# Making the weight sums of a seven-product FFN on the vector engine instead of by accumulating transfers

## The chip, the cores and the metric

The kernel runs on one core of a Trainium2 chip. That core has a matrix engine (PE, which also loads its own weights, shown as PEld), a vector engine (DVE), an activation engine (ACT), a general engine (POOL), a sequencer that mainly starts transfers (SP), and 16 DMA engines that move data between HBM and the on-chip memory. The metric is the device time of one execution in microseconds.

## The reference

Two residual layers over a sequence of 512 tokens with 1024 channels, each followed by a dense SwiGLU FFN. The FFN is the part that matters here:

```
def swiglu_layer(x, norm_g, w_gate_up, w_down):
    h = rmsnorm(x, norm_g)
    g, u = jnp.split(h @ w_gate_up, 2, axis=-1)     # 1024 -> 2 x 2816
    return x + (jax.nn.silu(g) * u) @ w_down        # 2816 -> 1024
```

All in float32. The first layer mixes by a recurrence and a state-space model, the second by attention; the change touches neither.

## The kernel before, in words

Channels lie on the 128 partitions and tokens along the free axis, so that an activation tile is 128x512. To reach float32 accuracy each operand is split into a high part (a cast on ACT, line 93) and a low part (a subtraction on DVE, line 94), and each product is three matmuls: low by high, high by low, high by high (lines 163 to 165). Both parts are tiles of up to 128x1024.

The FFN has 22 hidden tiles. They are worked off in three parts, of 8, 7 and 7 tiles (`HID`); after each part comes its down-projection of eight output tiles (lines 838 to 842). The first five hidden tiles of a layer are made by ordinary products. Tiles 5 to 21, in this text *pairs* (a gate tile and an up tile), are made by `seven`: the pair of weight tiles and the activations are seen as 2x2 blocks, and seven block products replace eight. So each layer has a stretch of 3 pairs and two stretches of 7 pairs, and there are 34 pairs in all. A block product is 4 x 3 = 12 matmuls of 256 columns, so a pair is 84 matmuls.

The weight side of the seven products needs, beside the gate tile itself (`a1`) and the right half of the up tile (`a22`), four sums: `s13` is a tile with two sums, and `s24` is made from `s13` and the gate tile by two additions (lines 143 and 144). In the kernel before, the two sums of `s13` are made on the way in: the left half of the up tile is loaded twice, into both halves of the tile (line 132), and then two transfers started by POOL add another block on top (lines 135 and 136). The gate tile comes by line 133 and `a22` by line 134. Each of the four weight tiles is then split into high and low by ACT and DVE.

`weight` makes the tiles ahead of their use: for pairs, four tiles ahead, which is one pair. Where the tiles lie is set by two rings (`ring`): four buffers for raw tiles inside an FFN (a pair takes two of them: the gate tile and `s13`), five for split tiles. `s24` has a single buffer, `a22` has two.

In `seven` the order of the products on PE is: B11 with `a1`; then the sixth product of the pair before (`end1`); T2 with `s24`; the seventh of the pair before (`end2`); T1 and T3 with `s13`; B21 with `a1`. Results are taken out of the accumulators by ACT and DVE between them: `s` and `m5` by ACT, `u2`, `u3`, `tg`, `tu` by DVE (lines 787 to 813). T3 is accumulated onto T2, so PE may start T3 only when `u2` (line 792) has read T2; in the same way the seventh product waits for `u3` (line 799).

Each engine works through its own queue strictly in order. The order inside a queue is not that of the source but is chosen by a list scheduler when the program is built, which also puts transfers where it expects their buffers to be free. An instruction of a queue that has to wait holds up everything behind it.

Of the kernel before, what the change touches and what calls it, by code (L numbers as in the profile page):

```python
# [10 lines left out]
F32 = mybir.dt.float32  # L11
# [3 lines left out]
ALU = mybir.AluOpType  # L15
AX = mybir.AxisListType

P = 128
# [7 lines left out]
KF = FF // P  # L26
# [3 lines left out]
NSTD = 5  # L30
# [31 lines left out]
def trunk(ctx: ExitStack, tc: tile.TileContext, a):  # L62
    nc = tc.nc
    mm = nc.tensor.matmul
    V, S, G = nc.vector, nc.scalar, nc.gpsimd
# [18 lines left out]
    WMAX = D  # L84
# [7 lines left out]
    def split(src, hi, lo, eng=V):  # L92
        S.copy(hi, src)  # L93
        eng.tensor_tensor(out=lo, in0=src, in1=hi.bitcast(F32), op=ALU.subtract)  # L94
# [4 lines left out]
    lent = {"stage": None, "pool": None, "raw": 0, "split": 0}  # L99

    def ring(what, stage):

        own, more = (NRAW, 1) if what == "raw" else (NSPL, 2)
        names = (("raw", F32),) if what == "raw" else (("whi", F32R), ("wlo", F32R))
        pool, bufs = wp, own
        if stage is not None and stage == lent["stage"]:
            lent[what] += 1
            if lent[what] % (own + more) >= own:
                pool, bufs = lent["pool"], more
        return [pool.tile([P, WMAX], dt, tag=n, bufs=bufs, name=n) for n, dt in names]  # L110

    parts = {}

    def emit(j):
        src, n, kind, stage = specs[j]
        HW = WMAX // 2
        if kind == "plain":
            raw, = ring("raw", stage)
            hi, lo = ring("split", stage)
            step = n if j else n // 4  # L120
            for c in range(0, n, step):
                nc.sync.dma_start(out=raw[:, c:c + step], in_=src[:, c:c + step])
                split(raw[:, c:c + step], hi[:, c:c + step], lo[:, c:c + step], G if src.tensor.name in on_pool else V)
        elif kind == "a1":

            g, u = src
            fp = lent["pool"]
            raw, = ring("raw", stage)
            s13, = ring("raw", stage)
            a22 = fp.tile([P, HW], F32, tag="a22", name="a22", bufs=2)  # L130
            for z in range(2):
                nc.sync.dma_start(out=s13[:, z * HW:(z + 1) * HW], in_=u[:, :HW])
            nc.sync.dma_start(out=raw, in_=g)
            nc.sync.dma_start(out=a22, in_=u[:, HW:])
            nc.gpsimd.dma_start(out=s13[:, :HW], in_=u[:, HW:], accum_op=ALU.add)  # L135
            nc.gpsimd.dma_start(out=s13[:, HW:], in_=g[:, :HW], accum_op=ALU.add)
            parts.update(raw=raw, s13=s13, a22=a22)
            hi, lo = ring("split", stage)
            split(raw, hi, lo)
        elif kind == "s24":  # L140
            raw, s13 = parts["raw"], parts["s13"]
            t = lent["pool"].tile([P, WMAX], F32, tag="s24", name="s24", bufs=1)
            V.tensor_tensor(out=t[:, :HW], in0=s13[:, :HW], in1=raw[:, :HW], op=ALU.add)  # L143
            V.tensor_tensor(out=t[:, HW:], in0=t[:, :HW], in1=raw[:, HW:], op=ALU.add)
            hi, lo = ring("split", stage)
            split(t, hi, lo)
        elif kind == "s13":
            hi, lo = ring("split", stage)
            split(parts["s13"], hi, lo)
        else:  # L150
            hi, lo = (lent["pool"].tile([P, HW], F32R, tag=f"a22{z}", name=f"a22{z}", bufs=1) for z in "hl")
            split(parts["a22"], hi, lo)
        w_of[j] = (hi, lo)

    def weight(i):
        while emitted[0] < len(specs) and emitted[0] <= i + (AHEAD if specs[emitted[0]][2] == "plain" else 4):
            emitted[0] += 1
            emit(emitted[0] - 1)
        return w_of.pop(i, None)
# [69 lines left out]
    def slot(i, dtype):  # L229
        return [xp.tile([P, T], dtype, tag=f"x{z}{i}", name=f"x{z}{i}") for z in "hl"]  # L230
# [79 lines left out]
    with ExitStack() as rctx:  # L310
# [63 lines left out]
        for c in range(NT):  # L374
# [33 lines left out]
            out=adt.rearrange("p (c h) -> p c h", c=NT),  # L408
            in0=dt.rearrange("p (c h) -> p c h", c=NT),
            scalar=-1.0,  # L410
            in1=ea.rearrange("p (o h) -> p o h", o=1).to_broadcast([P, NT, H]),
# [24 lines left out]
        for g in range(2):  # L436
# [7 lines left out]
            for c in range(NT):  # L444
                s = slice(c * P, (c + 1) * P)
# [3 lines left out]
                out=t.rearrange("p (c l) -> p c l", c=NT), in0=ps.rearrange("p (c l) -> p c l", c=NT),  # L449
                in1=tri.rearrange("p (o l) -> p o l", o=1).to_broadcast([P, NT, P]), op=ALU.mult,  # L450
# [245 lines left out]
        op = rctx.enter_context(tc.tile_pool(name="op", bufs=1))  # L696
# [9 lines left out]

    HOMES = [("F", i) for i in range(5)] + [("S", i) for i in (8, 9, 10, 11, 4, 5, 6, 7)] + [("F", i) for i in range(5)] + [("S", i) for i in (8, 9, 10, 11)]

# [4 lines left out]
    def ffn(norm, idx, after):  # L717
        l, gu, dn = idx
        HT = T // 2
        with ExitStack() as fctx:  # L720
            fp = fctx.enter_context(tc.tile_pool(name="fp", bufs=1))
# [47 lines left out]
            def finish(m, tu):  # L769
                z, i = HOMES[m]  # L770
                hi, lo = slot(i, F32R) if z == "S" else [fp.tile([P, T], F32R, tag=f"a{y}{i}", name=f"a{y}") for y in "hl"]
                split(tu, hi, lo)
                act[m] = (hi, lo)

            def small(tag):
                return fp.tile([P, HT], F32, tag=tag, name=tag, bufs=2)

            def seven(m, last):

# [2 lines left out]
                r1, r2 = (pa.tile([P, T], F32, tag="pa", name="ps_r")[:, :HT] for _ in range(2))  # L782
                r3 = pm.tile([P, T], F32, tag="pm", name="ps_r3")[:, :HT]
                s, u2, u3, m5 = small("s"), small("u2"), small("u3"), small("m5")
                a1 = weight(gu[m]["a1"])
                product(r1, a1, 0, "B11", True)
# [64 lines left out]
    with ExitStack() as actx:  # L851
# [11 lines left out]
        for w, (gn, rn, scale) in enumerate((("q_gain", "q_rope", 0.125), ("k_gain", "k_rope", 1.0))):  # L863
            g = am.tile([P, 1], F32, name=f"gain{w}", bufs=1)
# [301 lines left out]
```

## Time and profile before

| | |
|---|---|
| median of 3 runs | 1334.52 us (1334.01 to 1335.09) |
| the profiled execution | 1333.48 us, of which the span from first to last instruction is 1331.6 us |
| PE busy | 1296.0 us, 97% of the span |
| DVE busy | 928.1 us, 70% |
| ACT busy | 645.6 us, 48% |
| POOL busy | 180.0 us, 14% |
| moved by DMA | 153.46 MB, mean 115 GB/s |

Busy shares are averages over stages with different limits. A busy PE only says that matmuls were in flight; whether it lost time is seen by comparing a stretch's length with that of the same work where nothing was waited for. In the rows below, `raw`, `s`, `u` and `a` are tile names without their numbers: `raw` is any tile of the raw ring (the gate tile and `s13`), `s<-raw` on line 143 is the first addition for `s24`, `wlo` is the low part of a weight tile, and `a` stands for `a22`.

### The profile page before, as it was taken

The numbers are of one execution on the slowest core, as the hardware profiler recorded it, in microseconds if no ns is written. First come the engines' busy times: TensorE is split into PE (matmuls) and PEld (weight loads), VectorE is DVE, ScalarE is ACT, GpSimd is POOL, SyncE is SP. The second block draws the span as 40 slices with busy tenths as digits, with TensorE's granted clock in tenths as the row PEclk, the third lists the DMA queues.
The fourth block names the chain that finished last, engine by engine and source line by source line (L and its number), as shares of the span: only waits on it lengthen the run. The fifth ranks groups of instructions, "written<-read, shape, count | busy, mean of one in ns | idle before, by whom it ended". The sixth has DMA issues, their size and how long they took to land.

```text
span 1331.6 us, 18948 instructions
## 1 busy us (share of the span) xinstructions
PE 1296.0 (97%) x7346; PEld 1113.9 (84%) x7346; DVE 928.1 (70%) x1550; ACT 645.6 (48%) x1012; POOL 180.0 (14%) x178
## 2 busy tenths in 40 slices
PE   7999989999999999999999999999999999999998
PEld 6877767788889889889888877877878989889997
DVE  6886789975688558747764666777789746765772
ACT  6743858443455325424443467546654514433540
POOL 0000000000010111011104453354201011111100
PEclk9999989999999999999999999999999999999999
DMA  7323322532454646564632321221245554565541
GB/s 242 112 80 94 96 74 70 163 111 91 143 131 109 173 109 164 162 143 111 158 96 80 95 79 33 64 79 49 66 132 120 158 127 127 144 162 131 148 128 56
DMA packets 58154, 153.46 MB, mean 115 GB/s; under 512 B 6464, under 2 KB 7232, under 8 KB 57936
## 3 DMA queue, kind: packets, MB, share of 16 engines
q1 hardware_dynamic: 48272, 134.43, 32.7%
q0 software_dynamic: 9792, 17.83, 8.6%
q8 instruction: 57, 0.93, 0.3%
q14 instruction: 33, 0.27, 0.1%
HBM read 150.10 MB, written 2.13 MB: 114 GB/s over the span
## 4 chain that ended last, share of the span: by engine, by line
PE 81%; DVE 8%; ACT 4%; DMA 4%; issue 2%; SPq 0%; POOL 0%; DVEq 0%; ACTq 0%; POOLq 0%
PE ps_pr L163 15%; PE ps_pr L164 15%; PE ps_pr L165 15%; PE ps_r L765 6%; PE ps_r L767 6%; PE ps_r L766 6%; DMA raw<-in_w_gu 4%; PE ps_qkv L905 3%; PE ps_qkv L906 3%; PE ps_qkv L907 3%; DVE wlo L94 3%; PE ps_pT L1017 1%; ACT s L996 1%; PE ps_s L988 1%; PE ps_o L1025 1%
## 5 line engine op out<-in xcount | busy, mean ns | idle before, releaser
L93 ACT CAST whi<-raw 128x1024 fp32r<-128x1024 f32 (+2 forms) x223 | 227.4, 1022 | 327.1 <-PE ps_pr L165 208.8
L163 PE MATMUL ps_pr<-xh,wlo 128*128 128x512 f32 x704 | 279.7, 397 | 13.0 <-DVE wlo L94 12.3
L164 PE MATMUL ps_pr<-xl,whi 128*128 128x512 f32 x704 | 277.7, 394 | 0.6 <-DVE xl L245 0.6
L165 PE MATMUL ps_pr<-xh,whi 128*128 128x512 f32 x704 | 276.6, 393 | 0.0
L94 DVE TENSOR_TENSOR wlo<-raw,whi 128x1024 fp32r<-128x1024 f32 (+2 forms) x191 | 224.4, 1181 | 42.1 <-ACT whi L93 41.2
L163 PEld LDWEIGHTS ps_pr<-xh,wlo 128*128 128x128 f32 x704 | 133.5, 190 | 42.4 <-DVE wlo L94 13.1
L164 PEld LDWEIGHTS ps_pr<-xl,whi 128*128 128x128 f32 x704 | 133.4, 189 | 29.7 <-DVE xl L245 1.8
L165 PEld LDWEIGHTS ps_pr<-xh,whi 128*128 128x128 f32 x704 | 133.3, 189 | 28.6 <-issue 0.6
L840 DVE TENSOR_TENSOR x<-ps_pr,x 128x512 f32<-128x512 f32 x48 | 33.2, 691 | 96.8 <-PE ps_pr L165 96.6
L94 POOL TENSOR_TENSOR wlo<-raw,whi 128x1024 fp32r<-128x1024 f32 x32 | 78.0, 2438 | 167.1 <-ACT whi L93 167.1
L135 POOL DMA_DIRECT2D raw<-in_w_gu x34 | 30.4, 893 | 482.8 <-DMA raw<-in_w_gu 191.8
L765 PE MATMUL ps_r<-xh,wlo 128*128 128x256 f32 x272 | 77.1, 283 | 0.0
L767 PE MATMUL ps_r<-xh,whi 128*128 128x256 f32 x272 | 77.0, 283 | 0.0
L766 PE MATMUL ps_r<-xl,whi 128*128 128x256 f32 x272 | 77.0, 283 | 0.0
L907 PE MATMUL ps_qkv<-whi,xh 128*128 128x512 f32 x192 | 75.5, 393 | 0.0
L905 PE MATMUL ps_qkv<-whi,xl 128*128 128x512 f32 x192 | 75.4, 392 | 0.0
L906 PE MATMUL ps_qkv<-wlo,xh 128*128 128x512 f32 x192 | 75.3, 392 | 0.0
L93 ACT CAST whi<-s 128x1024 fp32r<-128x1024 f32 x34 | 35.8, 1052 | 71.2 <-PE ps_pr L165 37.4
L143 DVE TENSOR_TENSOR s<-raw 128x512 f32<-128x512 f32 x34 | 23.5, 691 | 56.3 <-DMA raw<-in_w_gu 54.5
L163 PE MATMUL ps_pr<-ah,wlo 128*128 128x512 f32 x160 | 62.3, 389 | 0.0
L164 PE MATMUL ps_pr<-al,whi 128*128 128x512 f32 x160 | 62.3, 389 | 0.0
L165 PE MATMUL ps_pr<-ah,whi 128*128 128x512 f32 x160 | 62.2, 389 | 0.0
(372 smaller groups left out, 3074.7 us busy)
## 6 DMA issues: line engine op xcount, KB each, us to landing
raw<-in_w_gu SPq DMA_DIRECT2D x54, 512.0 KB, 3.6
raw<-in_w_in SPq DMA_DIRECT2D x35, 512.0 KB, 3.6
raw<-in_w_gu SPq DMA_DIRECT2D x68, 256.0 KB, 3.4
raw<-in_w_gu POOLq DMA_DIRECT2D x68, 256.0 KB, 5.5
raw<-in_w_dn SPq DMA_DIRECT2D x32, 448.0 KB, 3.9
raw<-in_w_qkv SPq DMA_DIRECT2D x24, 512.0 KB, 3.5
a<-in_w_gu SPq DMA_DIRECT2D x34, 256.0 KB, 3.9
raw<-in_w_out SPq DMA_DIRECT2D x16, 512.0 KB, 3.6
```

The source lines that it names most:

```text
L93: S.copy(hi, src)
L94: eng.tensor_tensor(out=lo, in0=src, in1=hi.bitcast(F32), op=ALU.subtract)
L163: mm(ps, lhsT=wl[ws], rhs=xh[xs], start=start, stop=False)
L164: mm(ps, lhsT=wh[ws], rhs=xl[xs], start=False, stop=False)
L165: mm(ps, lhsT=wh[ws], rhs=xh[xs], start=False, stop=stop)
L765: mm(ps, lhsT=wl[:, c:c + P], rhs=fh, start=first and k == 0, stop=False, skip_group_check=not first)
L766: mm(ps, lhsT=wh[:, c:c + P], rhs=fl, start=False, stop=False, skip_group_check=not first)
L767: mm(ps, lhsT=wh[:, c:c + P], rhs=fh, start=False, stop=k == 3, skip_group_check=not first)
L840: V.tensor_tensor(out=x[m], in0=ps, in1=x[m], op=ALU.add)
L905: mm(pss[t], lhsT=xl[:, ts_], rhs=wh[:, cols], start=(k == 0), stop=False)
L906: mm(pss[t], lhsT=xh[:, ts_], rhs=wl[:, cols], start=False, stop=False)
L907: mm(pss[t], lhsT=xh[:, ts_], rhs=wh[:, cols], start=False, stop=(k == KD - 1))
```

## The change

The two accumulating transfers per pair go, and so do the two loads of the up tile's left half and the separate load of its right half. Instead the up tile is loaded whole by one transfer, into the ring place that `s13` had. `s13` becomes a tile of its own with a single buffer, and DVE makes its two sums by two more additions of 128x512 in front of the two that make `s24`. The five `F` homes of activation tiles become four, and `u2`, `u3` and `m5` have one buffer each instead of two.

```diff
@@ emit, kind "a1" @@
             raw, = ring("raw", stage)
-            s13, = ring("raw", stage)
-            a22 = fp.tile([P, HW], F32, tag="a22", name="a22", bufs=2)
-            for z in range(2):
-                nc.sync.dma_start(out=s13[:, z * HW:(z + 1) * HW], in_=u[:, :HW])
+            up, = ring("raw", stage)
             nc.sync.dma_start(out=raw, in_=g)
-            nc.sync.dma_start(out=a22, in_=u[:, HW:])
-            nc.gpsimd.dma_start(out=s13[:, :HW], in_=u[:, HW:], accum_op=ALU.add)
-            nc.gpsimd.dma_start(out=s13[:, HW:], in_=g[:, :HW], accum_op=ALU.add)
-            parts.update(raw=raw, s13=s13, a22=a22)
+            nc.sync.dma_start(out=up, in_=u)
+            a22 = up[:, HW:]
+            s13 = lent["pool"].tile([P, WMAX], F32, tag="s13", name="s13", bufs=1)
+            parts.update(raw=raw, s13=s13, a21=up[:, :HW], a22=a22)
@@ emit, kind "s24" @@
+            V.tensor_tensor(out=s13[:, :HW], in0=a21, in1=a22, op=ALU.add)
+            V.tensor_tensor(out=s13[:, HW:], in0=a21, in1=raw[:, :HW], op=ALU.add)
             t = lent["pool"].tile([P, WMAX], F32, tag="s24", name="s24", bufs=1)
             V.tensor_tensor(out=t[:, :HW], in0=s13[:, :HW], in1=raw[:, :HW], op=ALU.add)
             V.tensor_tensor(out=t[:, HW:], in0=t[:, :HW], in1=raw[:, HW:], op=ALU.add)
@@ homes and small results @@
-    HOMES = [("F", i) for i in range(5)] + ... + [("F", i) for i in range(5)] + ...
+    HOMES = [("F", i) for i in range(4)] + ... + [("F", i) for i in range(3)] + ... + [("F", i) for i in range(4)]
-                return fp.tile([P, HT], F32, tag=tag, name=tag, bufs=2)
+                return fp.tile([P, HT], F32, tag=tag, name=tag, bufs=2 if tag == "s" else 1)
```

In the changed kernel the gate tile is loaded by line 129, the up tile by line 130, and the four additions are lines 139, 140, 142 and 143; `u2`, `u3` and `tg` are lines 794, 801 and 809.

On DVE, the place is the first layer's first 7-pair stretch, where its fifth pair ends and its sixth begins; here the tiles of the seventh are made (`raw_4755` is its `s13`, `raw_4754` its gate tile). `a22l` is the low part of the fifth pair's `a22`, `xl6` an activation's low part, and `wlo_4698` belongs to the sixth pair's `s13`. Before:

```order
L94 TENSOR_TENSOR a22l_4594<-a22_4486,a22h_4593 128x512
L143 TENSOR_TENSOR s24_4794<-raw_4755,raw_4754 128x512
L94 TENSOR_TENSOR xl6_4694<-tu_4476,xh6_4693 128x512
L799 TENSOR_TENSOR u3_4617<-ps_r_4613,s_4615 128x256
L144 TENSOR_TENSOR s24_4794<-s24_4794,raw_4754 128x512
L800 TENSOR_TENSOR tu_4611<-m5_4618,u3_4617 128x256
L94 TENSOR_TENSOR wlo_4798<-s24_4794,whi_4797 128x1024
L94 TENSOR_TENSOR wlo_4698<-raw_4620,whi_4697 128x1024
L807 TENSOR_TENSOR tg_4610<-ps_r3_4614,u2_4616 128x256
L94 TENSOR_TENSOR wlo_4764<-raw_4754,whi_4763 128x1024
L792 TENSOR_TENSOR u2_4751<-ps_r_4748,s_4750 128x256
```

The same place on DVE after the change; `raw_4737` is the seventh pair's whole up tile, `raw_4736` its gate tile, `raw_4471` the up tile of the fifth, `s13_4607` the sums of the sixth:

```order
L94 TENSOR_TENSOR a22l_4578<-raw_4471,a22h_4577 128x512
L94 TENSOR_TENSOR xl7_4676<-tu_4462,xh7_4675 128x512
L801 TENSOR_TENSOR u3_4601<-ps_r_4597,s_4599 128x256
L802 TENSOR_TENSOR tu_4595<-m5_4602,u3_4601 128x256
L94 TENSOR_TENSOR wlo_4680<-s13_4607,whi_4679 128x1024
L139 TENSOR_TENSOR s13_4740<-raw_4737 128x512
L809 TENSOR_TENSOR tg_4594<-ps_r3_4598,u2_4600 128x256
L140 TENSOR_TENSOR s13_4740<-raw_4737,raw_4736 128x512
L142 TENSOR_TENSOR s24_4774<-s13_4740,raw_4736 128x512
L94 TENSOR_TENSOR wlo_4742<-raw_4736,whi_4741 128x1024
L143 TENSOR_TENSOR s24_4774<-s24_4774,raw_4736 128x512
L794 TENSOR_TENSOR u2_4733<-ps_r_4730,s_4732 128x256
```

The first addition that needs a transfer has moved behind `u3`, `tu` and the split of the sixth pair's `s13`, whose single buffer it writes; all four additions now stand in front of `u2`, where before the second one stood in front of `u3` already.

On SP, the transfers of the same stretch's last pairs; `L132` fills the two halves of an `s13` tile. Before:

```order
L133 DMA raw_4484<-in_w_gu 128x1024
L134 DMA a22_4351<-in_w_gu 128x512
L132 DMA raw_4485<-in_w_gu 128x512 x2
L132 DMA raw_4620<-in_w_gu 128x512 x2
L134 DMA a22_4486<-in_w_gu 128x512
L133 DMA raw_4754<-in_w_gu 128x1024
L133 DMA raw_4619<-in_w_gu 128x1024
L134 DMA a22_4621<-in_w_gu 128x512
L132 DMA raw_4755<-in_w_gu 128x512 x2
```

After, where `L129` is a gate tile and `L130` an up tile, for the last four pairs:

```order
L129 DMA raw_4337<-in_w_gu 128x1024
L129 DMA raw_4470<-in_w_gu 128x1024
L130 DMA raw_4338<-in_w_gu 128x1024
L130 DMA raw_4471<-in_w_gu 128x1024
L129 DMA raw_4603<-in_w_gu 128x1024
L129 DMA raw_4736<-in_w_gu 128x1024
L130 DMA raw_4604<-in_w_gu 128x1024
L130 DMA raw_4737<-in_w_gu 128x1024
```

Two transfers per pair stand on SP where there were four, and POOL, which had two per pair, has none in the FFN. An up tile's place in the ring becomes free only when the right half of the up tile two pairs earlier has been split (`a22l`), so its transfer starts there.

## Rows read from the trace of the kernel before

**Rows 1.** The page: busy time, share of the span and instructions.

```profile
PE 1296.0 (97%) x7346; PEld 1113.9 (84%) x7346; DVE 928.1 (70%) x1550; ACT 645.6 (48%) x1012; POOL 180.0 (14%) x178
```

**Rows 2.** Pair stretches: length; busy PE, PEld, DVE, ACT, POOL; clock, DMA share, GB/s.

```profile
413.20:443.43 30.23, 30.23 (x253) 30.23 (x252) 23.53 (x34) 17.00 (x26) 0.00 (x0) 1.00 0.43 126
486.98:560.20 73.22, 71.05 (x589) 70.64 (x588) 55.10 (x85) 37.94 (x61) 7.04 (x8) 1.00 0.58 150
598.31:673.69 75.38, 72.27 (x589) 70.97 (x588) 54.87 (x85) 37.49 (x61) 7.07 (x8) 1.00 0.51 131
1027.63:1057.87 30.24, 30.24 (x254) 30.23 (x253) 23.36 (x34) 16.98 (x26) 1.77 (x2) 1.00 0.53 143
1101.41:1177.27 75.86, 72.96 (x590) 72.14 (x589) 55.08 (x85) 37.40 (x61) 7.07 (x8) 0.98 0.54 137
1215.37:1289.69 74.32, 71.82 (x589) 70.80 (x588) 55.02 (x85) 38.02 (x61) 7.06 (x8) 1.00 0.58 144
```

**Rows 3.** Waits: who for whom, us in total, times, longest.

```profile
PE ps_r L765 <- DVE wlo L94: 7.5, 4, 2.5
PE ps_r L765 <- DVE u L799: 1.7, 2, 1.3
...
DVE s L143 <- DMA raw<-in_w_gu: 54.5, 21, 5.4
```

**Rows 4.** Timeline of DVE: start, us, instruction, idle before and releaser.

```profile
634.49 0.68 DVE L94 TENSOR_TENSOR a22l<-a,a22h 128x512 fp32r<-128x512 f32 x1
640.54 0.69 DVE L143 TENSOR_TENSOR s<-raw 128x512 f32<-128x512 f32 x1 [5.36 <-DMA raw<-in_w_gu]
...
641.75 0.42 DVE L799 TENSOR_TENSOR u<-ps_r,s 128x256 f32<-128x256 f32 x1
...
643.02 2.35 DVE L94 TENSOR_TENSOR wlo<-raw,whi 128x1024 fp32r<-128x1024 f32 x2
```

**Rows 5.** Timeline of POOL at the same place.

```profile
634.95 0.88 POOL L135 DMA_DIRECT2D raw<-in_w_gu  x1 [18.91 <-DVE tu L813]
```

**Rows 6.** Timeline of PE at the same place.

```profile
642.22 0.39 PE L765 MATMUL ps_r<-t10h,a22l 128*128 128x256 f32 x1 [1.27 <-DVE u L799]
...
645.42 0.39 PE L765 MATMUL ps_r<-t00h,wlo 128*128 128x256 f32 x1 [1.50 <-DVE wlo L94]
```

**Rows 7.** Busy time by stretch, behind the longest stop of PE.

```profile
1149.40:1152.80 3.40, 3.40 (x17) 3.19 (x17) 2.15 (x5) 0.91 (x3) 0.00 (x0) 0.51 0.76 240
```

**Rows 8.** Timeline of DVE in a pair of the first 7-pair stretch.

```profile
525.17 0.68 DVE L144 TENSOR_TENSOR s<-s,raw 128x512 f32<-128x512 f32 x1
525.77 0.41 DVE L799 TENSOR_TENSOR u<-ps_r,s 128x256 f32<-128x256 f32 x1
526.10 0.68 DVE L94 TENSOR_TENSOR xl<-tu,xh 128x512 fp32r<-128x512 f32 x1
...
527.04 2.35 DVE L94 TENSOR_TENSOR wlo<-raw,whi 128x1024 fp32r<-128x1024 f32 x2
529.31 0.41 DVE L807 TENSOR_TENSOR tg<-ps_r,u 128x256 f32<-128x256 f32 x1
```

**Rows 9.** Groups of DVE by form: count, busy us, mean ns, idle before.

```profile
L94 DVE TENSOR_TENSOR wlo<-raw,whi 128x1024 fp32r<-128x1024 f32 x155 | 188.2, 1220 | 33.9 <-ACT whi L93 33.4
...
L144 DVE TENSOR_TENSOR s<-s,raw 128x512 f32<-128x512 f32 x34 | 23.3, 685 | 0.3
```

**Rows 10.** DMA issues: queue, count, KB each, median us to landing.

```profile
raw<-in_w_gu SPq DMA_DIRECT2D x68, 256.0 KB, 3.4
raw<-in_w_gu POOLq DMA_DIRECT2D x68, 256.0 KB, 5.5
```

**Rows 11.** Line 133, the gate tiles of the pairs, 512 KB each.

```profile
DMA to landing us min/median/max: 3.4/3.9/6.6
```

**Rows 12.** Busy time by stretch: the ordinary hidden tiles of each layer.

```profile
363.00:413.20 50.20, 50.20 (x227) 41.69 (x227) 44.37 (x74) 25.35 (x37) 7.47 (x7) 1.00 0.52 133
970.00:1027.63 57.63, 56.96 (x256) 46.33 (x255) 50.55 (x82) 29.65 (x42) 5.04 (x5) 1.00 0.43 118
```

More of the change, by code (lines that the diff above doesn't have):

```diff
@@ L126, in emit @@
             g, u = src
-            fp = lent["pool"]
             raw, = ring("raw", stage)
-            s13, = ring("raw", stage)
-            a22 = fp.tile([P, HW], F32, tag="a22", name="a22", bufs=2)
-            for z in range(2):
-                nc.sync.dma_start(out=s13[:, z * HW:(z + 1) * HW], in_=u[:, :HW])
+            up, = ring("raw", stage)
             nc.sync.dma_start(out=raw, in_=g)
-            nc.sync.dma_start(out=a22, in_=u[:, HW:])
-            nc.gpsimd.dma_start(out=s13[:, :HW], in_=u[:, HW:], accum_op=ALU.add)
-            nc.gpsimd.dma_start(out=s13[:, HW:], in_=g[:, :HW], accum_op=ALU.add)
-            parts.update(raw=raw, s13=s13, a22=a22)
+            nc.sync.dma_start(out=up, in_=u)
+            a22 = up[:, HW:]
+            s13 = lent["pool"].tile([P, WMAX], F32, tag="s13", name="s13", bufs=1)
+            parts.update(raw=raw, s13=s13, a21=up[:, :HW], a22=a22)
             hi, lo = ring("split", stage)
@@ L140, in emit @@
         elif kind == "s24":
-            raw, s13 = parts["raw"], parts["s13"]
+            raw, s13, a22 = parts["raw"], parts["s13"], parts["a22"]
+            a21 = parts["a21"]
+            V.tensor_tensor(out=s13[:, :HW], in0=a21, in1=a22, op=ALU.add)
+            V.tensor_tensor(out=s13[:, HW:], in0=a21, in1=raw[:, :HW], op=ALU.add)
             t = lent["pool"].tile([P, WMAX], F32, tag="s24", name="s24", bufs=1)
@@ L705, in trunk @@
             norm.feed(m)
-    HOMES = [("F", i) for i in range(5)] + [("S", i) for i in (8, 9, 10, 11, 4, 5, 6, 7)] + [("F", i) for i in range(5)] + [("S", i) for i in (8, 9, 10, 11)]
+    NF = NSTD - 1
+    HOMES = [("F", i) for i in range(NF)] + [("S", i) for i in (8, 9, 10, 11, 4, 5, 6, 7)] + [("F", i) for i in range(3)]
+    HOMES += [("S", i) for i in (8, 9, 10, 11)] + [("F", i) for i in range(NF)]
+    assert len(HOMES) >= KF
     def ffn(norm, idx, after):
```

## The prediction, made before the changed kernel ran

> **What bounds the kernel now.** I read the busy times first. PE is busy for 97% of the span, DVE for 70%, POOL for 14% [rows 1]. The change takes no matmul away, so it can only win where PE stands still, and the busy times by stretch show where. A 3-pair stretch takes 30.23 us and its PE is never idle [rows 2], so a pair costs PE 10.08 us and seven pairs 70.56. The four 7-pair stretches take 73.22, 75.38, 75.86 and 74.32 us: they lose 2.66, 4.82, 5.30 and 3.76 us, together 16.54. The stretches of ordinary tiles ahead of them leave PE idle for 0.67 us, all of it in the second layer [rows 12]. So 16.5 us, 1.2% of the run, is what stands to be won.
>
> The waits name the cause from the other end. PE waits for `wlo` (7.5 us) and for `u3` (1.7 us), both made by DVE; DVE, before the first addition for `s24`, waits 54.5 us in 21 waits for a transfer into the raw ring [rows 3]. One place shows the chain. POOL starts an accumulating transfer at 634.95 [rows 5], as late as that because its destination had to be free and then loaded. DVE has finished `a22l` at 635.2 and stands until 640.54 behind that transfer, 5.36 us; `u3`, for which PE's result has long been ready, is queued behind the addition and comes at 641.75, and the low parts of two weight tiles at 643.02 [rows 4]. PE stops twice, until 642.22 for `u3` and until 645.42 for `wlo` [rows 6]. So PE stops not because DVE is full but because DVE's queue stands still behind a late transfer. Once the stop is long it costs twice: after the longest one, near 1149.4, the granted clock is 0.51 for 3.40 us, that is, the lower level of 1.2 GHz, and 17 matmuls run there where 28 would at 0.12 us each [rows 7]. That is 17 x 0.12 = 2.04 us of work, so 1.4 of the 5.30 us of that stretch are clock.
>
> **The change part by part.** *Transfers.* The chain for one `s13` is now a load (median 3.4 us) and then an accumulation (5.5 us) [rows 10], 8.9 us in a row after the buffer is free. It becomes one 512 KB load; the gate tiles are of that size and land in 3.9 us in the middle, 3.4 to 6.6 [rows 11]. That is 5.0 us less. But the buffer comes free later: the up tile's right half is split last of the four tiles, and the next-but-one pair's load starts only behind that `a22l`. I compared the work that stands on DVE between `a22l` and the addition that needs this load, for the sixteen pairs in the 7-pair stretches that are loaded inside them, priced by the spacing of starts in a busy pair: 0.60 us for 128x512, 0.33 for 128x256, 2.27 / 2 = 1.14 for 128x1024 [rows 8]. Six pairs have 5.3 to 5.6 us of such work, three have 4.5, three 3.55, one 3.0 and three 2.4. Against 3.9 us, nine wait for nothing and seven wait 3 x 0.35 + 0.9 + 3 x 1.5 = 6.5 us in all. Those waits replace most of the 54.5 us.
>
> *Two more additions per pair,* 68 in all, of 128x512. They are 0.685 us each [rows 9], 0.60 by start to start, so 34 x 1.2 = 41 us more on DVE. In a pair DVE now has three splits of 1.14, five instructions of 0.60 and five of 0.335, that is 3.42 + 3.00 + 1.68 = 8.1 us; with the additions 9.3, and about 9.6 because three instructions read what the one in front wrote and can't overlap it. PE needs 10.08 for the same pair, so DVE's cover is 0.5 us per pair. It is thin, but PE still sets the pace.
>
> *Does DVE come in time inside the pair?* The tightest date is `u2`: T2 ends three products (3 x 1.44 = 4.32 us) into the pair, and T3, which needs `u2` done, starts after five, at 7.2. In the new order DVE starts the first addition after the pair's beginning, then does `tg`, which PE's second product makes ready at about 3.0, so the addition starts at 2.4 at the earliest; then two additions, one split in some pairs, and `u2`, which ends 2.6 us behind the first addition, or 3.7 with the split: at 5.0 to 6.1. That leaves 1.1 to 2.2 us before PE would stop. A pair that waits 1.5 us for its load eats that, and gets 0.5 back in each pair that doesn't wait. The other dates (`s24` before T2, `s13` before T1 of the next pair) lie further out, 3 to 4 us.
>
> *What is left of the stops.* If every new wait of DVE fits into that room, nothing; if none does, all 6.5 us. I take 3, near the middle, since three of the four stretches have a pair with the 1.5 us wait and most others none.
>
> *The stretches before the pairs.* The ordinary tiles share DVE with the making of the activation operands: 44.37 of 50.20 us and 50.55 of 57.63 [rows 12]. Up to five more 128x512 instructions fall there, 3.0 us, and DVE's idle time of 5.8 and 7.1 covers them: nothing. Without that cover it would be 3.0 us in each layer.
>
> *Homes, single buffers, POOL.* `u2` is read by `tg` before the next pair's `u2` is written on the same engine, `u3` right away, `m5` a whole pair before the next: nothing, and a stop of under 0.4 us per pair, one 128x256 instruction, if that were wrong. The homes that move are ones whose reader, a down-projection or the last ordinary product, has ended. POOL loses 68 transfers and nobody waits for it in the FFN.
>
> *Sum.* 1333.48 for the profiled execution, minus 16.54, plus 3.0: 1319.9. The median of the runs shown lies 1.04 above that execution, so **1321.0** on their scale.
>
> **A rule that speaks against it.** Starts of 128x512 instructions in a busy pair lie 0.60 us apart though each lasts 0.68 [rows 8]. The Trainium skill ("VectorE: DVE Perf Modes", section "The DRAIN you can't avoid") says that the next instruction does not start until the pipe of the one before is empty. By that rule the starts would lie a full duration apart; the trace shows them overlapping by 0.08 us, so it is not borne out as written. By the trace the sum is the one above, by the rule that of the first rival below.
>
> **The rivals.** *DVE becomes the bound, mildly.* If in the new order most instructions depend on the one in front and don't overlap, a pair costs full durations: four additions at 0.69, three splits at 1.22 [rows 9], `a22l`, `tu` and `xl` at 0.69, five of 0.42 [rows 8]: 2.8 + 3.7 + 2.1 + 2.1 = 10.6 us, 0.5 more than PE. Five pairs of each long stretch prepare another pair, so 4 x 5 x 0.5 = 10 us come back, and the time is 1334.5 - 16.5 + 10 = 1328. For it: the additions do form a chain. Against: the scheduler puts other instructions between them.
>
> *Slower: the up tile's load becomes the late transfer, in front of `u2`.* The additions stand in front of `u2` and `u3` in the queue as they did, and the load starts later than now. If it took 6.6 us, the longest of its kind [rows 11], DVE would wait 6 x 1.2 + 3 x 2.1 + 3 x 3.1 + 3.6 + 3 x 4.2 = 39 us, of which 16 x 0.5 + 4 x 1.5 = 14 fit into DVE's room: 25 us of stops, 1334.5 - 16.5 + 25 = 1343. From 6.1 us on this outweighs the win. For it: the 6.6 us was seen, and two loads often go together on SP. Against: the median is 3.9, under a DMA load that included three quarters of a megabyte per pair which is now gone.
>
> *The change doesn't reach the stops.* If PE's stops come from the split's place in the queue and not from the transfer, they stay: 1334 to 1336. Against it stand the 5.36 us of DVE idle time that a transfer ends, right before two stops [rows 4, 6].
>
> **How the numbers follow.** The forecast gets 0.60, its own range is 1318 (no stop left) to 1324.5 (all 6.5 us lost). DVE as the bound gets 0.18, the unreached stops 0.10, the slower case 0.12. The measurement can tell about 0.2% from no change, 2.7 us here. Faster by more than that are the first two cases and a little of the third: 0.79; within it, 0.09; slower, 0.12. The range that should hold the time 8 times in 10 runs from 1315.5, a little below the case in which all is won and the second layer's start gains too, to 1331, beyond the second case.
>
> **What would show it.** Right: the four long stretches of pairs last 70.6 to 72 us; DVE's wait for the raw ring falls from 54.5 us to under 12; DVE is busy some 40 us longer; PE's waits for `wlo` are gone; the granted clock stays at 1.00 in all of them. DVE as the bound shows as `wlo` being waited for while DVE is never idle; the late load shows as DVE idle in front of line 139, followed by PE stops that `u2` ends. I am wrong in the core if the long stretches still take 73 us or more although DVE no longer waits for transfers.

## The result, and the profile after

The changed kernel takes 1317.41 us in the median of four runs (1317.09 to 1317.60), the kernel before 1334.80 in the same comparison: a ratio of 0.9862, with a 95% interval of 0.9838 to 0.9886. That is faster, by 17.4 us; 1321.0 had been forecast, with 1318 to 1324.5 as the forecast's own range, so the size lies 0.6 us beyond its favourable end.

The page of the changed kernel, its busy times:

```profile
PE 1290.4 (98%) x7346; PEld 1111.8 (84%) x7346; DVE 967.2 (74%) x1618; ACT 645.6 (49%) x1012; POOL 120.0 (9%) x110
```

DVE has 68 instructions and 39.1 us more than before, POOL 68 instructions and 60 us less [rows 1]. That PE is busy 5.6 us *less* with the same 7346 matmuls is no contradiction. Inside a pair the matmuls overlap: each is recorded with 0.28 us, but they start 0.12 us apart, and only these 0.12 us add to the busy time. The last one before a stop adds its whole 0.28 us, and 17 at the lower clock add 3.40 us [rows 7].

Busy time by stretch of the changed kernel, the six stretches of pairs (columns as in [rows 2]):

```profile
413.25:443.63 30.38, 30.38 (x253) 30.28 (x252) 24.90 (x38) 16.72 (x26) 0.00 (x0) 1.00 0.37 107
487.18:557.73 70.55, 70.55 (x589) 70.55 (x588) 60.72 (x95) 37.89 (x61) 0.00 (x0) 1.00 0.31 95
595.84:666.39 70.55, 70.55 (x589) 70.55 (x588) 61.13 (x95) 38.16 (x61) 0.00 (x0) 1.00 0.31 96
1020.40:1050.78 30.38, 30.38 (x253) 30.28 (x252) 24.50 (x37) 16.42 (x26) 0.00 (x0) 1.00 0.34 105
1094.33:1164.88 70.55, 70.55 (x589) 70.55 (x588) 61.27 (x95) 37.90 (x61) 0.00 (x0) 1.00 0.32 95
1202.99:1273.54 70.55, 70.55 (x589) 70.55 (x588) 60.33 (x93) 37.83 (x61) 0.00 (x0) 1.00 0.30 96
```

The four long stretches took 73.22, 75.38, 75.86 and 74.32 us [rows 2] and take 70.55 each: 16.58 us won, to the last stop. DVE now fills 60.3 to 61.3 of the 70.55 us instead of 55, and PE does not feel it. Each 3-pair stretch is 0.15 us longer. The profiled execution went from 1333.48 to 1317.52, 15.96 us; the six stretches account for 16.29, and some 0.3 us are lost again elsewhere.

DVE's waits in the changed kernel from the first pair to the end of the last (who for whom, us in total, times, longest), and the wait for `u3` in the same part of the kernel before:

```profile
DVE u L801 <- PE ps_r L769: 14.8, 12, 2.4
...
DVE s L139 <- DMA raw<-in_w_gu: 0.6, 2, 0.3
```

```profile
DVE u L799 <- PE ps_r L767: 10.1, 13, 1.7
```

The wait for the raw ring, 54.5 us in 21 waits [rows 3], is 0.6 us in two, and both lie in the down-projections, at 568 and 1175 us. DVE's wait for PE at `u3` grew from 10.1 to 14.8 us; over `u2`, `u3`, `tg` and `tu` DVE waited for PE in both kernels for about 21 us. Of PE's waits for `wlo` and `u3` in the pairs none is left.

DVE's timeline in a loaded pair of the first long stretch, with SP's load in front of it (start, us, instruction):

```profile
523.48 7.37 SPq L130 DMA_DIRECT2D raw<-in_w_gu  x2
...
522.77 0.68 DVE L94 TENSOR_TENSOR a22l<-raw,a22h 128x512 fp32r<-128x512 f32 x1
523.37 0.68 DVE L94 TENSOR_TENSOR xl<-tu,xh 128x512 fp32r<-128x512 f32 x1
523.97 0.42 DVE L801 TENSOR_TENSOR u<-ps_r,s 128x256 f32<-128x256 f32 x1
524.49 0.42 DVE L802 TENSOR_TENSOR tu<-m,u 128x256 f32<-128x256 f32 x1
...
527.30 0.69 DVE L139 TENSOR_TENSOR s<-raw 128x512 f32<-128x512 f32 x1
527.91 0.42 DVE L809 TENSOR_TENSOR tg<-ps_r,u 128x256 f32<-128x256 f32 x1
528.24 0.68 DVE L140 TENSOR_TENSOR s<-raw 128x512 f32<-128x512 f32 x1
528.84 0.69 DVE L142 TENSOR_TENSOR s<-s,raw 128x512 f32<-128x512 f32 x1
529.44 0.42 DVE L794 TENSOR_TENSOR u<-ps_r,s 128x256 f32<-128x256 f32 x1
529.77 0.68 DVE L143 TENSOR_TENSOR s<-s,raw 128x512 f32<-128x512 f32 x1
```

The load for the next pair's up tile is issued at 523.48, right behind the `a22l` that frees its buffer, and the first addition reads it at 527.30, 3.82 us later, with no wait between (the view merges this load with the next one, at 530.52). The scheduler put `tg` between the two halves of `s13` and `u2` between those of `s24`, so that no addition follows the one whose result it reads.

### The profile page after: what moved, and what is told of

It is laid out like the page before. It is cut to its first block, busy times and chain, and to the rows that moved or that the text cites. A ratio compares the mean times of both kernels' runs of the same rounds, so it can differ in the third digit from the quotient of the medians.

```text
span 1315.7 us, 18691 instructions
## 1 busy us (share of the span) xinstructions
PE 1290.4 (98%) x7346; PEld 1111.8 (84%) x7346; DVE 967.2 (74%) x1618; ACT 645.6 (49%) x1012; POOL 120.0 (9%) x110
## 4 chain that ended last, share of the span: by engine, by line
PE 90%; ACT 4%; DVE 4%; issue 1%; DMA 1%; SPq 0%; POOL 0%; DVEq 0%; ACTq 0%
PE ps_pr L162 15%; PE ps_pr L163 15%; PE ps_pr L164 15%; PE ps_r L767 9%; PE ps_r L769 9%; PE ps_r L768 9%; PE ps_qkv L907 3%; PE ps_qkv L908 3%; PE ps_qkv L909 3%; PE ps_pT L1019 1%; ACT s L998 1%; PE ps_s L990 1%; PE ps_o L1027 1%; PE ps_ao L164 1%; PE ps_o L1028 1%
## 5 line engine op out<-in xcount | busy, mean ns | idle before, releaser
L93 ACT CAST whi<-raw 128x1024 fp32r<-128x1024 f32 (+2 forms) x189 | 191.6, 1018 | 312.0 <-PE ps_pr L164 181.0
L94 DVE TENSOR_TENSOR wlo<-raw,whi 128x1024 fp32r<-128x1024 f32 (+2 forms) x157 | 184.1, 1174 | 37.9 <-ACT whi L93 36.8
L93 ACT CAST whi<-s 128x1024 fp32r<-128x1024 f32 x68 | 71.4, 1050 | 83.5 <-PE ps_pr L164 49.7
L94 DVE TENSOR_TENSOR wlo<-s,whi 128x1024 fp32r<-128x1024 f32 x68 | 83.1, 1221 | 15.8 <-ACT whi L93 15.8
L767 PEld LDWEIGHTS ps_r<-xh,wlo 128*128 128x128 f32 x272 | 52.2, 192 | 0.0
```

The lines of the kernel that those rows point to most:

```text
L767: mm(ps, lhsT=wl[:, c:c + P], rhs=fh, start=first and k == 0, stop=False, skip_group_check=not first)
```

## The experiments

Each kernel ran beside the kernel before on the same chip; the medians are of runs of that comparison. The kernel before had medians of 1333.67 to 1335.25 us there, so a difference between two kernels of different comparisons is good to some 1.6 us. Theory A is the prediction's: the accumulating transfer was the late link, it stopped DVE's queue, and through it PE.

**1. Homes and single buffers alone.** The kernel before with the second and third part of the change and without the first:

```
-    HOMES = [("F", i) for i in range(5)] + ...
+    NF = NSTD - 1
+    HOMES = [("F", i) for i in range(NF)] + ...
-                return fp.tile([P, HT], F32, tag=tag, name=tag, bufs=2)
+                return fp.tile([P, HT], F32, tag=tag, name=tag, bufs=2 if tag == "s" else 1)
```

> Only the four F homes and the single buffers of u2, u3, m5 are taken over; the sums come by accumulating transfers as before. Theory A (PE's stops come from DVE's first addition for s24 standing behind a late accumulating transfer): nothing changes, 1333 to 1336 us, the four long pair stretches together lose 15 to 18 us against 70.56 each, DVE's wait for the raw ring stays near 54 us. Theory B (the room that was freed, or the order that it gives, makes the win): most of the 17 us appear here, under 1325 us.

Measured: 1335.76 us, ratio 1.0000 (0.9984 to 1.0016). DVE's wait in this kernel:

```profile
DVE s L143 <- DMA raw<-in_w_gu: 53.0, 20, 6.2
```

Nothing moved: 53.0 us in 20 waits, against 54.5 in 21 [rows 3]; the four long stretches lose 18.1 us against 70.56 each, just above the 15 to 18 expected. The freed room is worth nothing by itself.

**2. The sums alone.** The other half: the first part of the change, with the old homes and double buffers.

```
-            s13, = ring("raw", stage)
+            up, = ring("raw", stage)
...
+            V.tensor_tensor(out=s13[:, :HW], in0=a21, in1=a22, op=ALU.add)
+            V.tensor_tensor(out=s13[:, HW:], in0=a21, in1=raw[:, :HW], op=ALU.add)
```

> All four sums on DVE from plain transfers, homes and small buffers as in the kernel before. Theory A: the whole win, 1316 to 1319 us, long stretches of 70.6 us each. Theory B: near 1334 us.

Measured: 1318.03 us, ratio 0.9863 (0.9838 to 0.9889); the long stretches are 70.55, 70.57, 70.55 and 70.63 us long. This is the whole win, within the noise. Experiments 1 and 2 together put it on the sums.

**3. The accumulation left out.** The kernel before without its two accumulating transfers; `s13` holds its loaded half only, so part of the weight sums is not computed.

```
-            nc.gpsimd.dma_start(out=s13[:, :HW], in_=u[:, HW:], accum_op=ALU.add)
-            nc.gpsimd.dma_start(out=s13[:, HW:], in_=g[:, :HW], accum_op=ALU.add)
```

> The kernel before with its two accumulating transfers per pair left out, so that s13 holds the up tile's left half twice and the sums are incomplete; nothing is added on DVE. Theory A: the chain in front of the first addition is 3.4 us of loading instead of 8.9, the stops go, 1317 to 1321 us, DVE's wait for the raw ring falls below 15 us. Theory C (the loads and their buffers are what is late, not the accumulation behind them): at least half of the stops stay, over 1326 us.

Measured: 1317.63 us, ratio 0.9864 (0.9841 to 0.9887).

```profile
DVE s L141 <- DMA raw<-in_w_gu: 8.7, 8, 2.9
```

The load of `s13` still comes late now and then, 8.7 us in all, and PE does not stop once: four stretches of 70.55 or 70.56 us. What made the stops was the second leg, the accumulation behind the load; whether by its lateness or by its mere presence, this run can't tell, and experiments 4, 7 and 9 can.

**4. The accumulation kept, its destination free early.** The kernel before with `s13` in three buffers of its own, outside the raw ring, which shrinks to three; the homes and single buffers of the change and two small filler tiles taken out make the room.

```
-            s13, = ring("raw", stage)
+            s13 = fp.tile([P, WMAX], F32, tag="s13", name="s13", bufs=3)
-        own, more = (NRAW, 1) if what == "raw" else (NSPL, 2)
+        own, more = (NRAW, 0) if what == "raw" else (NSPL, 2)
```

> The sums still come by accumulating transfers, but s13 has three buffers of its own instead of two places in the raw ring (which shrinks to three, for gate tiles alone), with the smaller homes and small buffers to make room, and two filler tiles left out. Theory A in its narrow form (the accumulation is late because its destination comes free late): load and accumulation start a pair earlier, the stops mostly go, 1318 to 1323 us, DVE's wait for the raw ring below 20 us. If accumulating transfers are the trouble however early they start: over 1329 us.

Measured: 1325.02 us, ratio 0.9913 (0.9884 to 0.9943), 2 us above theory A's upper end. Of the 54.5 us of waiting 4.4 are left, and in the four long stretches of pairs PE stands once, for 0.6 us. So 68 accumulating transfers can be had almost without a stop, if their buffer is free early. The 7.6 us that this kernel lies above the changed one are outside the pairs. The timeline of the largest such place, in a down-projection, of ACT, DVE and PE (idle before, and releaser, in brackets), and the busy time right behind it:

```profile
1053.54 1.05 ACT L92 CAST whi<-raw 128x1024 fp32r<-128x1024 f32 x1 [3.90 <-DMA raw<-in_w_dn]
...
1054.62 2.45 DVE L93 TENSOR_TENSOR wlo<-raw,whi 128x1024 fp32r<-128x1024 f32 x2 [3.35 <-ACT whi L92]
...
1060.77 0.51 PE L162 MATMUL ps_pr<-xh,wlo 128*128 128x512 f32 x1 [1.36 <-ACT xh L92]
```

```profile
1061.40:1065.00 3.60, 3.50 (x9) 2.72 (x10) 1.96 (x3) 1.04 (x1) 0.00 (x0) 0.55 0.35 134
```

The chain is the old one with another tile in it: a down tile lands late, ACT's cast waits 3.90 us for it, DVE's split 3.35 us for the cast, `tu` and its high part `xh` fall behind, and PE stops for 1.36 us. Then it runs at a granted clock of 0.55, mostly the lower level of 1.2 GHz, for another 3.6 us. This down-projection takes 47.92 us, against 44.45 in kernel 9, which keeps four raw buffers. So some 3.5 of the 7.6 us are such a late tile; that the smaller ring made it late is likely and was not tested by itself. Much of the rest kernel 9 has too, and a part of it is another pace of the matmuls (last section).

**5 and 6. DVE given more to do.** The changed kernel with two or four further additions per pair in front of the sums for `s24`; their results are overwritten by the real ones.

```
+            V.tensor_tensor(out=t[:, HW:], in0=a21, in1=a22, op=ALU.add)
+            V.tensor_tensor(out=t[:, :HW], in0=a21, in1=a22, op=ALU.add)
```

> The changed kernel with two further 128x512 additions per pair, whose results are overwritten by the real ones, in front of the sums for s24 (68 instructions, 41 us of DVE at 0.60 us each). Theory A (DVE's queue has room; the win was the late transfer): DVE is busy 60.7 of 70.55 us in a long stretch, 9.8 us idle for seven pairs; five of them carry the additions, 6.0 us, so the room is just enough on average: 1317.5 to 1320, long stretches 70.55 to 71. Rival, DVE at its edge as the prediction's pair model has it (9.6 of 10.08 us, so 10.8 with the two): 0.7 us per loaded pair, 4 x 5 x 0.7 = 14 us, 1327 to 1333, long stretches 73 to 75, with PE waiting for wlo or u2.

> The changed kernel with four further 128x512 additions per pair at the same place (136 instructions, 82 us of DVE). Both theories expect a loss here and differ in its size. Theory A: 12.0 us more in a long stretch against 9.8 us idle, so 2 to 4 us per long stretch: 1326 to 1334. Rival, DVE at its edge (12.0 us per loaded pair against 10.08): 4 x 5 x 1.9 = 38 us, 1350 to 1358. If u2 is what comes late first (2.4 us more in front of it, against the predicted margin of 1.1 to 2.2), PE's waits name u2 and not wlo.

Measured: 1321.25 us with two (ratio 0.9900, 0.9873 to 0.9926) and 1329.36 with four (0.9960, 0.9945 to 0.9975), 3.8 and 12.0 us above the changed kernel. Busy time of the longest 7-pair stretch with two more, and PE's waits with four:

```profile
487.44:558.82 71.38, 71.26 (x589) 70.77 (x588) 65.51 (x104) 37.63 (x61) 0.00 (x0) 1.00 0.30 93
```

```profile
PE ps_r L771 <- DVE u L798: 3.6, 6, 1.1
PE ps_r L771 <- DVE wlo L94: 1.4, 2, 0.7
```

With two, the four long stretches lose 0.83, 0.18, 0.03 and 0.30 us, 1.3 in all; the rest comes from the down-projections between them, 1.7 us from the one in front of the last long stretch. With four, PE does wait, mostly for `u2` (line 798), the date that the prediction called the tightest. Theory A's estimate for four holds; for two it was a little low, and the model of an engine at its edge asks for three to four times the loss measured in both. What counted here is DVE's idle time over the whole stretch, 9.8 of 70.55 us, and not the half microsecond of a loaded pair: the additions ran into it and it absorbed 6 us nearly whole.

**7, 8 and 9. Half of the accumulation back.** The changed kernel with one half of `s13` made by load and accumulation again, the other half on DVE: 34 accumulating transfers instead of 68 or none. In 7 it is the left half, which an addition for `s24` reads, in 8 the right half, which nothing reads before the split of `s13`; `s13` has two buffers. 9 is 7 with three, for which two small filler tiles give the room.

```
-            s13 = lent["pool"].tile([P, WMAX], F32, tag="s13", name="s13", bufs=1)
+            s13 = lent["pool"].tile([P, WMAX], F32, tag="s13", name="s13", bufs=2)
+            nc.sync.dma_start(out=s13[:, :HW], in_=u[:, :HW])
+            nc.gpsimd.dma_start(out=s13[:, :HW], in_=u[:, HW:], accum_op=ALU.add)
...
-            V.tensor_tensor(out=s13[:, :HW], in0=a21, in1=a22, op=ALU.add)
```

> The changed kernel, but the left half of s13 (which the first addition for s24 reads) is made again by a load and an accumulating transfer, with two buffers for s13; the right half stays on DVE. Theory A (a late accumulation in front of that addition stops DVE's queue, and so u2, u3 and wlo): stops come back in part, 1322 to 1334, DVE waits 10 us or more for the transfer in that line. Rival (the number of accumulating transfers is what counts, half of them half the loss): 1325 to 1327, the same as the run with the right half. Rival (two buffers are early enough): 1317 to 1319, no waits.

> The changed kernel, but the right half of s13 (which nothing reads before the split of s13, a product later) is made by a load and an accumulating transfer, with two buffers for s13; the left half stays on DVE. Theory A (what counts is the place in DVE's queue of the first reader): 1317 to 1322, DVE's wait in front of the split under 5 us. Rival (the number of accumulating transfers counts): 1325 to 1327, the same as the run with the left half.

> The run with the left half accumulated, but with three buffers for s13 instead of two (two small filler tiles give the room); the number of accumulating transfers, their sizes and the first reader's place on DVE are unchanged. Theory A (the accumulation cost 49 us there only because its destination came free late, at the split of s13 two pairs earlier; load 2.9 us and accumulation 5.0 us then end behind the addition that reads them): most of it comes back, 1317 to 1325, DVE's wait for the accumulation under 8 us. Rival (the accumulating transfers themselves are what costs, at whatever time they start): 1345 or more. Rival (half of them, half the loss): 1325 to 1327.

Measured: 7 takes 1366.52 us (ratio 1.0232, 1.0204 to 1.0261), 8 takes 1324.34 (0.9914, 0.9885 to 0.9944), 9 takes 1321.37 (0.9907, 0.9890 to 0.9925). Kernel 7 takes 33 us more than the kernel before, with half as many accumulations, far outside what any theory expected. DVE's wait at the addition, the first long stretch, and a timeline of POOL's issue and DVE:

```profile
DVE s L143 <- DMA s<-in_w_gu: 53.5, 17, 5.8
```

```profile
487.91:567.95 80.04, 74.85 (x590) 73.79 (x589) 57.77 (x89) 38.02 (x61) 5.22 (x6) 0.96 0.47 124
```

```profile
501.12 0.86 POOL L134 DMA_DIRECT2D s<-in_w_gu  x1 [17.59 <-DVE u L795]
...
502.20 0.69 DVE L94 TENSOR_TENSOR a22l<-raw,a22h 128x512 fp32r<-128x512 f32 x1
506.32 0.69 DVE L143 TENSOR_TENSOR s<-s,raw 128x512 f32<-128x512 f32 x1 [3.44 <-DMA s<-in_w_gu]
506.93 0.69 DVE L94 TENSOR_TENSOR xl<-tu,xh 128x512 fp32r<-128x512 f32 x1
507.54 0.42 DVE L802 TENSOR_TENSOR u<-ps_r,s 128x256 f32<-128x256 f32 x1
```

This is [rows 4] again: DVE stands for 3.44 us at the addition, and the low part `xl` and `u3`, both ready, stand behind it. The accumulation lands 5.0 us after its issue in the median of this kernel, and only 4 to 7.5 us lie between issue and addition for the pairs loaded inside the long stretches, where the load before it had to wait for the split of `s13` two pairs earlier. The size of the loss is explained in part only. DVE waits for the accumulations about as long as in the kernel before, 53.5 against 54.5 us, and 21.4 us more for plain loads, but the long stretches lose 46.4 us instead of 16.58: PE's waits for DVE's results in the pairs grow from 10.0 to 30.4 us, and the granted clock of the four stretches falls to 0.96 and 0.98. Why DVE's waits, longer by a third, cost nearly three times as much was not tested. In 9 the same two instructions are further apart:

```profile
503.02 0.88 POOL L133 DMA_DIRECT2D s<-in_w_gu  x1 [17.58 <-DVE u L793]
...
516.02 0.68 DVE L142 TENSOR_TENSOR s<-s,raw 128x512 f32<-128x512 f32 x1
```

13.0 us here, 6.7 or more in every pair, and no wait for an accumulation is left. One buffer more brings back 45 of the 49 us; the number and size of the transfers did not change. (Kernel 9 also runs its matmuls at another pace, worth 1.1 us per long stretch, see the last section; the stretches of 7 are 11 to 14 us longer than those of 9.) So the rival by which accumulations cost by their number falls, in 7 and in 9: 34 of them cost 49, 7 or 4 us.

Kernel 8 came out above theory A's range, and 0.7 us below that of the rival by number, so alone it doesn't tell the two apart. Nobody waits for its accumulation. Its waits, DVE's and PE's, and the longest of them, with SP's load and DVE:

```profile
DVE s L141 <- DMA raw<-in_w_gu: 17.9, 15, 3.6
...
PE ps_r L768 <- DVE u L795: 3.8, 5, 1.2
```

```profile
622.85 0.69 DVE L94 TENSOR_TENSOR a22l<-raw,a22h 128x512 fp32r<-128x512 f32 x1
...
623.56 0.33 SPq L130 DMA_DIRECT2D raw<-in_w_gu  x1
...
629.13 0.69 DVE L141 TENSOR_TENSOR s<-raw 128x512 f32<-128x512 f32 x1 [3.59 <-DMA raw<-in_w_gu]
```

The up tile comes late: its load starts as `a22l` ends and takes 5.5 us, and DVE stands 3.59 us at the first addition. The eight waits of 1 us and more, 15.4 of the 17.9 us, all follow a load that started 0.03 us behind an `a22l`. PE then waits for `u2` (line 795 here), and the four long stretches lose 5.7 us; in the profiled execution another 3.7 us are lost in a down-projection. This is the prediction's slower rival in a mild form, with the signs that it gave. Such loads land later here than in the changed kernel, after 4.1 us in the median instead of 3.7; why the order on DVE leaves them less time was not looked into.

**10. Loads later.** The changed kernel with three raw buffers instead of four.

```
-        own, more = (NRAW, 1) if what == "raw" else (NSPL, 2)
+        own, more = (NRAW, 0) if what == "raw" else (NSPL, 2)
```

> The changed kernel with three raw buffers in place of four, which makes every load of a gate, up or down tile start later; no instruction is added or taken away. This is a dose of the late load that the prediction's slower rival needed. Theory A (after the change the loads come with little to spare: the shortest lead from a load's issue to the addition in the changed kernel is 3.65 us, against 3.4 to 5.2 for its landing): DVE waits 5 to 25 us for the ring, but 9.8 us of room per long stretch takes most of it: 1319 to 1327. Rival (loads are not near any limit): 1317 to 1318.5, no new wait. Rival (late loads stop PE as the late accumulations did): 1330 to 1345.

Measured: 1319.93 us, ratio 0.9902 (0.9886 to 0.9918). One long stretch is longer, the other three are not:

```profile
1095.36:1167.46 72.10, 70.83 (x589) 70.62 (x588) 61.12 (x95) 37.55 (x61) 0.00 (x0) 1.00 0.31 94
```

```profile
PE ps_r L767 <- DVE u L794: 1.3, 1, 1.3
...
DVE s L139 <- DMA raw<-in_w_gu: 3.2, 6, 1.1
```

DVE's wait for the up tile grows from 0.6 to 3.2 us, less than expected, and PE stops once, for `u2`, 1.5 us of stretch. The margin of the loads is there and is small. In the changed kernel itself four loads inside the long stretches land less than 0.1 us before their addition starts.

## Why the prediction was right, step by step

*What stops PE.* Right, and shown from both sides: without the accumulation no stop is left (experiment 3), with it and its buffer early 0.6 and 1.5 us of PE's waits (4, 9), with its buffer late more than ever (7).

*The 16.54 us.* Right: 16.58 came from the long stretches.

*The wait for the up tile, 6.5 us, and the 3 us of stops left.* This is the term that was mis-sized: 0.6 us of waits, and no stop in the long stretches. Three things were wrong in it. The walk over DVE's queue added up the spacing of starts of an undisturbed pair and found 2.4 to 5.6 us between `a22l` and the addition; in the trace it is 2.6 to 5.7 us, because DVE also waits for PE and ACT on the way. The walk also took all sixteen loads inside the long stretches to start behind an `a22l`. Eight do, and have 3.83 to 5.67 us from issue to addition. The other eight, among them the four with the least time in the walk, start within 0.1 us of the end of `L143`, the last addition and the last reader of a gate tile, and have 5.7 to 7.3 us. One of them:

```profile
510.03 0.68 DVE L143 TENSOR_TENSOR s<-s,raw 128x512 f32<-128x512 f32 x1
...
510.77 0.33 SPq L130 DMA_DIRECT2D raw<-in_w_gu  x1
```

So it doesn't hold for half of these loads that an up tile's place becomes free only with `a22l`. And up-tile loads land after 3.4 us at least, 3.7 in the middle, 5.2 at most:

```profile
DMA to landing us min/median/max: 3.4/3.7/5.2
```

The gate tiles had shown 6.6 at most [rows 11]. And if the waits had come, they need not have cost half of their length: kernel 9 has 34 us of DVE waiting for the ring, and PE waits 1.5 us for it.

```profile
DVE s L140 <- DMA raw<-in_w_gu: 25.5, 19, 2.6
DVE s L142 <- DMA raw<-in_w_gu: 8.6, 4, 2.6
...
PE ps_r L766 <- DVE u L793: 1.5, 2, 0.8
```

With that term at nothing, the sum would have been 1316.94 on the profile's scale against 1317.52 measured. The difference is 0.3 us in the two 3-pair stretches and 0.3 behind the last long stretch; in front of the pairs it is 0.1, so "nothing" for the ordinary tiles was right within that.

*The tightest date.* `u2` is where the changed kernel still loses time, a little: both 3-pair stretches lose their 0.15 us at one matmul that starts when `u2` is done, here at 418.45 instead of 418.41, and runs 0.39 us.

```profile
417.98 0.42 DVE L794 TENSOR_TENSOR u<-ps_r,s 128x256 f32<-128x256 f32 x1
...
418.45 0.39 PE L767 MATMUL ps_r<-t10h,wlo 128*128 128x256 f32 x1
```

The next one starts 0.22 us later instead of 0.12. A margin of 1.1 to 2.2 us had been predicted; in these two pairs it was used up.

*DVE's price.* 41 us were forecast, 39.1 more were busy. A full pair goes from the `L140` at 616.60 to that at 626.74 in the second long stretch with 0.6 us of idle time in it: 9.5 us, where 9.3 to 9.6 had been worked out. The rival that priced 10.6 us per loaded pair at 10 us of loss was wrong in the price even where a pair is made that long: in experiment 5 a loaded pair has 9.5 + 1.2 us, and the cost is 3.8 us.

*The overlap of starts.* In the timeline above, `xl` starts 0.60 us behind `a22l`, which lasts 0.68, and `L802` starts 0.52 us behind `L801`, which lasts only 0.42 and whose result it reads. Independent neighbours overlap, dependent ones stand apart by more than the duration: L801 to an `L802` right behind it is 0.52 or 0.53 in all 12 cases between 413 and 700 us. The Trainium skill ("VectorE: DVE Perf Modes", section "The DRAIN you can't avoid") says that the next instruction does not start before the pipe is empty, and that one which is not held starts earlier; the prediction took up the first half alone. The trace shows the wait for the dependent neighbours and the overlap for the others. So each of the four additions of a chain cost 0.60 us once other work was put between them.

*The slower rival* (a late up-tile load) did not happen; experiments 8 and 10 made it happen in part, at 7 and 2.5 us. The 25 us it was given were for loads of 6.6 us, and no up tile took more than 5.5 in the changed kernel, 8 and 10.

*Not settled:* what part of the loss outside the pairs in kernels 4 and 9 comes from the two filler tiles that were taken out there, and why kernel 7 loses as much as it does.

## What to carry to other kernels

Look at what stands *behind* a waiting instruction in an engine's queue: an engine that is busy for 70% of the time stopped PE here, because one instruction that waited for a transfer held back three whose inputs were ready. Against such a wait, work on an engine with idle time can be the cheaper way to make a value, and its room is to be counted over the whole stretch that can absorb it, not over the densest step. A transfer of two legs into one buffer needs its destination free two landings ahead. Here one buffer more was worth 45 us (7 and 9), while half the transfers with a late buffer made the kernel slower (7).

## What the runs showed of the hardware

An accumulating transfer of 256 KB, started by POOL, takes clearly longer than a plain one of the same size, started by SP, in the same kernel (7; median from issue to landing):

```profile
s<-in_w_gu POOLq DMA_DIRECT2D x34, 256.0 KB, 5.0
s<-in_w_gu SPq DMA_DIRECT2D x32, 256.0 KB, 2.9
```

A plain load of twice the size lands after 3.7 us. No kernel here has a plain transfer of this kind on POOL, so how much of the difference is the accumulation and how much POOL's queue stays open.

In kernels 4 and 9, which lack the two filler tiles and keep `s13` in three buffers, and in no other, the matmuls ran at another pace with the granted clock at 1.00. Kernel 9, its first down-projection and its first long stretch, both without a stop:

```profile
445.55:489.78 44.23, 44.23 (x194) 36.02 (x193) 21.60 (x27) 9.01 (x10) 0.86 (x1) 1.00 0.38 114
489.78:559.24 69.46, 69.46 (x590) 69.46 (x589) 57.80 (x88) 37.99 (x61) 5.23 (x6) 1.00 0.54 142
```

The changed kernel takes 43.55 and 70.55 us for the same work. So 70.55 us is no floor for seven pairs, and the 7.6 and 4.0 us that kernels 4 and 9 lie above the changed one are a larger loss outside the pairs less a gain inside them. What shifts the pace was not tested.
